# A trunk of four mixers and 32 experts: the scan's input projection on PSUM's two idle banks, and the last norm on VectorE alone

## The chip, the cores and the metric

The kernel runs on one core of a Trainium2 chip. The metric is device time in microseconds (us) of one execution. Engines: PE is TensorE (PEld its weight loads), DVE is VectorE, ACT is ScalarE, POOL is GpSimd, SP is SyncE; a "q" behind a name is that engine's instruction queue (SPq L269 issues most weight loads).

## The reference

One layer, 256 tokens of width 1024, float32. Four branches mix the tokens, a gated sum merges them, and a sparse layer of 32 experts (top 4 of 32, weights of 1024 x 2048 and 1024 x 1024 for each expert) follows. Both sub-layers end in a layer norm.

```
proj   = x @ W_in                       # columns go to the branches and gates
br0    = sparse attention(q, ckv, ...)  # ckv = rms_norm(latents); index scores
                                        # relu(q_idx . k_idx) weighted per head,
                                        # the top 64 keys of each query
br1    = gate_b * conv3(gate_c * u)
br2    = s5 scan(u_scan)                # 32 groups of 16 channels, 64 complex states
br3    = 4-head attention into 256 memory tokens
h      = LN(alpha * x + (sum_r sigmoid(g_r) * (br_r @ W_branch[r])) @ W_o)
out    = LN(alpha * h + MoE(h))         # LN: (y - mu) * rsqrt(var + eps) * g + b
```

## The kernel before

The program is written as generators for the branches (`main`, `select`, `scan_part`, `memory` and others) that are advanced in turn. A scheduler then sets the order of the instructions on each engine from its own costs, so an edit in one place can move instructions in others. The order on an engine is fixed when the program is built; at run time each instruction waits for its inputs and for a free buffer, and everything behind it on its engine waits with it.

There are two long stages. In the dense stage (0 to about 400 us of the span) the projections are computed with the token block as the moving operand. Weights come as float32 by DMA, 1 MB at a time; each piece of 1024 x 128 is split by ScalarE (L320) and VectorE (L325) into a high and a low part, and each product takes three matmuls of 256 columns (`mm3`, L386 to L388), 8 times over, so that 24 matmuls make one half of a tile `[128, 512]`. Between them stand the small matmuls of the branches. In the expert stage (about 400 to 1300 us) 16 pairs of experts are streamed: L1500 and L1518 multiply, L1529 and L1530 scatter the result back to the tokens, L1534 adds it up.

All matmul results lie in PSUM, which has 8 banks of 512 float32 columns in each partition. The kernel hands them out by three pools that go round: `P` has 4 banks, `PT` (transposes) 2, and `PD` 2. The names that matter here:

- `pckv` (L1036, two tiles of `P`): the latents of the sparse attention before their norm. ScalarE computes the root of their mean square (L1039, result `rr`), VectorE inverts it (L1044) and multiplies it in (L1046, `latents()`), TensorE transposes the result (`pct`, L1051).
- `prl` (L820, tiles of `P`): index scores of `select`, taken through a Relu by ScalarE (L825), weighted and summed by VectorE (L832, L834); L840 and L841 find the largest.
- `pu` (L386 to L388, copied out by L1059): the scan's input projection, two tiles of two halves each, 96 matmuls in all. `projs` (L956) takes the bank from `P`. The generator calls `latents()` after the first tile.
- `warm` (L417), the only user of `PD` before the projection; the next is `pkt` (L696, L697) of `scan_part`, which comes behind it on TensorE.
- `scan_part` in four parts: `pkt`, `pe` (transposes, L707, copied out by ScalarE at L708), `pV` (L719, copied at L722), then VectorE's rotation and scan (L724 to L730), `py` (copied out at L747). Two parts run interleaved.
- `memory`: `pml` (scores), VectorE's row maximum (L926, L927), ScalarE's exponent (L929), VectorE's division (L931, L933), transposes `pmt` (copied out at L941), `pmo` (L945, product with the values).
- The tail: after the last pair VectorE aggregates the moments (L1745), ScalarE takes a root (L1746), VectorE inverts it (L1747) and forms `nm` (L1748). The output is four blocks of 128 rows x 512 columns. In each, VectorE takes columns 0 to 399 (`LNV`) in two operations (L1755, L1759); ScalarE normalises the other 112 (L1756) and GpSimd multiplies by the gain (L1757) and adds the bias (L1758). Each block leaves by its own DMA (L1760).

Of the kernel before, what the change touches and what calls it, by code (L numbers as in the profile page):

```python
# [13 lines left out]
FT = mybir.dt.float32  # L14
# [3 lines left out]
AF = mybir.ActivationFunctionType  # L18
OP = mybir.AluOpType
# [11 lines left out]
SC = 8  # L31
# [22 lines left out]
PLACES_AT = 3  # L54
ROWS_AT, SPLIT_AT = 1, 5
RESID = 4
LNV = 400
POOL_MIN = 4096
AHEAD = 2
AHEAD_W = 1  # L60
# [111 lines left out]
def tile_trunk(ctx, tc, a, out):  # L172
    nc = tc.nc
    PE, V, S, G = nc.tensor, nc.vector, nc.scalar, nc.gpsimd
# [5 lines left out]
    keep = ctx.enter_context(tc.tile_pool(name="keep", bufs=1))  # L180
# [10 lines left out]
    def P(nm):  # L191
        return ps.tile([128, 512], FT, name=nm, tag="pp", bufs=4)

    def PT(nm):
        return ps.tile([128, 512], FT, name=nm, tag="pt", bufs=2)

    def PD(nm):
        return ps.tile([128, 512], FT, name=nm, tag="pd", bufs=2)
# [161 lines left out]
    def take(i, half=None):  # L360
        unit = i, None if i in whole else half
        at = split_order.index(unit)
        n = AHEAD_W if i in whole else AHEAD
        for j in split_order[at:at + 1 + n]:
            if j not in ready:
                ready[j] = W(*j)
        return ready[unit] if half == unit[1] else Half(ready[unit], half)
# [22 lines left out]
    def projT(dst, w, c0, xx, m=128):  # L390
        for k in range(w.k):
            mm3(dst, w.h[:, k, c0:c0 + m], w.l[:, k, c0:c0 + m], xx.h[:, k, :], xx.l[:, k, :], k == 0, k == w.k - 1)
# [61 lines left out]
    def small(shape, nm, bufs=2):  # L454
        return keep.tile(shape, FT, name=nm, bufs=bufs)
# [71 lines left out]
    p = PT("pvc")  # L527
# [425 lines left out]
        res["br3"] = oX  # L953


    def projs(ids, xx, nm, put):  # L956
        for c, i in enumerate(ids):
            p = P(nm)
            for j in range(2):
                w = take(i, j)  # L960
                projT(p[:, j * 256:(j + 1) * 256], w, 0, xx)
                w.done()
            put(c, p)
            yield
# [4 lines left out]
    def main():  # L969
        res["kTm"] = B(128, MH, T)  # L970
        for c, _ in enumerate(projs(ID_K, mT, "pk", copy_to(res["kTm"]))):
            if c == 0:
                norm_in()
            yield
        vM = B(128, 2, MH * MD)
        for c, i in enumerate(ID_V):
            w = take(i)
            p = P("pv")
# [25 lines left out]
        p = P("pqi")  # L1004
# [9 lines left out]
        p = P("pki")  # L1014
# [16 lines left out]
        ss, r = small([128, 2], "ss", 1), small([128, 2], "rr", 1)  # L1031
        pl_ = [P("pckv") for _ in range(2)]
        for b in range(2):
            o = pl_[b][:, :136]
# [8 lines left out]
        def latents():  # L1043
            V.reciprocal(r, r)  # L1044
            for b in range(2):
                V.scalar_tensor_tensor(ckv.ap[:, b, :], pl_[b][:, :LAT], r[:, b:b + 1], kvg.ap, op0=OP.mult, op1=OP.mult)  # L1046
            for t in (wcw, kvg, sq, hF):
                t.free()
            p = PT("pct")
            for b in range(2):  # L1050
                PE.transpose(p[:, b * 128:(b + 1) * 128], ckv.ap[:, b, :], ident)  # L1051
            S.copy(ckvT.ap, p[:, :T])
            res.update(ckv=ckv, ckvT=ckvT)
# [4 lines left out]
        res.update(io_blk=io_blk, U=U, io2=carve(io_blk[1], (128, SC, 8, GN), *[(128, 8, GN), (128, 8, NJ + 1)] * 2))  # L1058
        for c, _ in enumerate(projs(ID_S, hX, "pu", lambda c, p: S.copy(  # L1059
                uP.ap[:, :, 2 * c:2 * c + 2, :].rearrange("p s m j -> p m j s"),  # L1060
                p.rearrange("p (m j s) -> p m j s", m=2, s=SC)))):
            if c == 0:
                latents()
            yield
        hN.free()
        res["uP"] = uP
        mqT = B(128, MH, T)
        yield from projs(ID_M, hX, "pmq", copy_to(mqT))
        res["mqT"] = mqT
        qT = B(128, 4, T)  # L1070
# [5 lines left out]
        for c2 in range(2):  # L1076
# [11 lines left out]
            for i in range(2):  # L1088
                c = c2 * 2 + i
                V.tensor_scalar(cv.ap[:, i, :], vv.ap[:, i, 0:T], cw(c, 0), cw(c, 3), op0=OP.mult,  # L1090
                                op1=OP.add)
                for k in (1, 2):
                    V.scalar_tensor_tensor(cv.ap[:, i, :], vv.ap[:, i, k:k + T], cw(c, k), cv.ap[:, i, :],
                                           op0=OP.mult, op1=OP.add)
# [8 lines left out]
        for n, r in enumerate((1, 3, 2, 0)):  # L1103
            if r == 2:
# [3 lines left out]
                for c in range(4):  # L1108
                    w = take(ID_GL, c // 2)
                    p = P("pgl")  # L1110
# [15 lines left out]
            for d2 in range(KC // 2):  # L1126
                p = P("pg")
# [7 lines left out]
                p = P("pbr")  # L1135
# [3 lines left out]
                m = mg.ap[:, 2 * d2:2 * d2 + 2, :].rearrange("p a t -> p (a t)")  # L1139
# [115 lines left out]
    for _ in main():  # L1255
        ahead()
        for nm in list(bgs):
            step(nm)
# [62 lines left out]
    for b in range(2):  # L1321
        mu, r, nm = mv1[:, b, 0:1], r1[:, b:b + 1], nm1[:, b:b + 1]
# [15 lines left out]
        p = PD("prk")  # L1338
# [401 lines left out]
                          {RESID: residual, RESID + 4: norm_rows}[e0]() if e0 in (RESID, RESID + 4) else None, e0 == 0, ln2 if final else None, after, behind, overflow)  # L1740
            ga = after

    mv2, r2, nm2 = keep.tile([128, 2, 2], FT, name="mv2"), small([128, 2], "r2", 1), small([128, 2], "nm2", 1)
    for b in range(2):
        V.bn_aggr(mv2[:, b], ln2[b].st)  # L1745
    S.activation(r2, mv2[:, :, 1], AF.Sqrt, bias=eps_t[:, 0:1], scale=1.0)  # L1746
    V.reciprocal(r2, r2)  # L1747
    V.scalar_tensor_tensor(nm2, mv2[:, :, 0], -1.0, r2, op0=OP.mult, op1=OP.mult)  # L1748
    for b in range(2):
        mu, r, nm = mv2[:, b, 0:1], r2[:, b:b + 1], nm2[:, b:b + 1]  # L1750
        for c in range(2):
            y = o = yacc[0].ap[:, b, c * 512:(c + 1) * 512]
            g_, b_ = (gb2[0].ap[:, i, c * 512:(c + 1) * 512] for i in range(2))
            va, vb = slice(0, LNV), slice(LNV, 512)
            V.scalar_tensor_tensor(o[:, va], y[:, va], mu, g_[:, va], op0=OP.subtract, op1=OP.mult)  # L1755
            S.activation(o[:, vb], y[:, vb], AF.Identity, bias=nm, scale=r)  # L1756
            G.tensor_tensor(o[:, vb], o[:, vb], g_[:, vb], op=OP.mult)  # L1757
            G.tensor_tensor(o[:, vb], o[:, vb], b_[:, vb], op=OP.add)  # L1758
            V.scalar_tensor_tensor(o[:, va], o[:, va], r, b_[:, va], op0=OP.mult, op1=OP.add)  # L1759
            nc.sync.dma_start(out[0, b * 128:(b + 1) * 128, c * 512:(c + 1) * 512], o)  # L1760


# [10 lines left out]
```

## Time and profile before

| what | value |
|---|---|
| time, median of 3 runs (lowest to highest) | 1317.6 us (1317.01 to 1318.38) |
| the profiled execution's own time, and its span | 1318.57 us, 1316.7 us |
| granted TensorE clock, mean over the span | 0.992 of 2.4 GHz |
| busy share of the span: PE, PEld, DVE, ACT, POOL | 92%, 51%, 36%, 24%, 8% |
| DMA over the span | 463.38 MB, mean 352 GB/s |

The rows below come from that one profiled execution. Times in them are microseconds from the start of the span. The busy shares are means over stages that are limited by different things, so a share of the whole span says little of one stage. Of a matmul the pitch (start of one to start of the next) tells what it costs in a row of matmuls, since they overlap: a 256-column matmul is listed with 0.28 us and starts every 0.12 us. The same holds for VectorE, whose operations are listed longer than their pitch.

### The profile page before, as it was taken

To read this page: it belongs to the slowest core of one execution; us is meant where nothing else is said; L and a number is where in the kernel's file an instruction comes from. 1 tells how busy PE (TensorE), PEld (TensorE's weight loads), DVE (VectorE), ACT (ScalarE), POOL (GpSimd) and SP (SyncE) were. 2 spreads that over 40 slices of the span, in tenths; PEclk is the share of its full clock that TensorE was granted. 3 is DMA by queue.
4 is the path that set the end of the run, shared out by engine and by line. 5 is a ranking of instruction groups with operands and counts; after the bars stand their busy time and mean duration, and the time that the engine had idled before them with its cause. 6 is when DMAs were issued, how large, how long until landed. Compare 5 with 4: busy or idle time off the path is not lost. (4 is left out here: it accounts for less than half of the span.)

```text
span 1316.7 us, 17368 instructions
## 1 busy us (share of the span) xinstructions
PE 1214.9 (92%) x6928; PEld 669.2 (51%) x6928; DVE 469.8 (36%) x972; ACT 319.6 (24%) x639; POOL 107.3 (8%) x158
## 2 busy tenths in 40 slices
PE   8799999999999999999999999898989898899984
PEld 8699999889853333333343333333333333333321
DVE  5896976755632133221212213021221212130214
ACT  4735545544422111011211102011010102020101
POOL 1103020246110000000000000000000000000001
PEclk9999999999999999999999999999999999999998
DMA  9816458974889999999999999999999999999993
GB/s 249 273 36 172 130 144 291 292 249 164 319 324 412 419 420 419 419 420 419 420 419 418 420 419 421 420 419 420 419 421 418 420 420 418 421 419 420 412 413 131
DMA packets 115238, 463.38 MB, mean 352 GB/s; under 512 B 19304, under 2 KB 54192, under 8 KB 68016
## 3 DMA queue, kind: packets, MB, share of 16 engines
q1 hardware_dynamic: 112512, 456.37, 87.6%
q0 software_dynamic: 2608, 5.83, 1.7%
q8 instruction: 57, 0.93, 0.3%
q14 instruction: 29, 0.24, 0.0%
q10 hardware_dynamic: 32, 0.01, 0.0%
HBM read 459.09 MB, written 3.08 MB: 351 GB/s over the span
## 5 line engine op out<-in xcount | busy, mean ns | idle before, releaser
L1500 PE MATMUL hp<-slab,slab 128*64 128x512 f32 x2048 | 484.7, 597 | 31.2 <-DMA slab<-in_w_up_dram 30.8
L1500 PEld LDWEIGHTS hp<-slab,slab 128*64 128x64 f32 x2048 | 157.6, 137 | 321.5 <-issue 238.5
L1518 PE MATMUL dp<-slab,slab 128*64 128x512 f32 x1024 | 232.3, 597 | 2.2 <-ACT slab L1515 1.2
L1518 PEld LDWEIGHTS dp<-slab,slab 128*64 128x64 f32 x1024 | 72.4, 137 | 127.3 <-issue 120.9
L325 DVE TENSOR_TENSOR slab<-slab,slab 128x1024 fp32r<-128x1024 f32 (+1 forms) x90 | 110.3, 1235 | 55.8 <-ACT slab L320 50.5
L320 ACT CAST slab<-slab 128x1024 fp32r<-128x1024 f32 x90 | 92.6, 1048 | 78.9 <-DMA slab<-in_w_in_dram 16.5
L1391 ACT ACTIVATE slab<-pxs,pcol 128x128 f32<-128x128 f32 x128 | 48.0, 457 | 235.2 <-PE pxs L1386 225.1
L1491 DVE CAST slab<-id 128x64 fp32r<-128x64 f32 x34 | 5.1, 192 | 221.3 <-PE hp L1494 212.5
L1377 POOL TENSOR_SCALAR slab<-slot_i,slot 128x64 f32<-128x64 f32 x32 | 13.9, 453 | 803.6 <-PE pta L1513 701.6
L388 PE MATMUL pg<-slab,slab 128*128 128x256 f32 x256 | 74.4, 291 | 0.0
L386 PE MATMUL pg<-slab,slab 128*128 128x256 f32 x256 | 74.3, 290 | 0.0
L387 PE MATMUL pg<-slab,slab 128*128 128x256 f32 x256 | 73.6, 288 | 0.0
L1386 PEld LDWEIGHTS pxs<-slab,slab 128*128 128x128 f32 x512 | 59.7, 192 | 25.7 <-issue 23.5
L1457 ACT CAST slab<-psg 128x256 fp32r<-128x256 f32 x16 | 6.0, 372 | 255.5 <-PE psg L1455 255.5
L1386 PE MATMUL pxs<-slab,slab 128*128 128x128 f32 x512 | 65.9, 282 | 1.1 <-DVE slab L1377 0.7
L1443 DVE TENSOR_SCALAR slab<-hp 128x256 f32<-128x256 f32 x64 | 27.0, 422 | 76.5 <-PE pta L1513 76.5
L1534 DVE TENSOR_TENSOR slab<-slab,psc 128x512 f32<-128x512 f32 x60 | 38.6, 684 | 43.7 <-PE psc L1530 43.7
L386 PEld LDWEIGHTS pg<-slab,slab 128*128 128x128 f32 x256 | 49.8, 194 | 2.0 <-issue 1.5
L388 PEld LDWEIGHTS pg<-slab,slab 128*128 128x128 f32 x256 | 49.9, 195 | 1.1 <-issue 1.1
L387 PEld LDWEIGHTS pg<-slab,slab 128*128 128x128 f32 x256 | 49.8, 194 | 0.3 <-issue 0.2
L1513 PE MATMUL pta<-ident,slab 128*128 128x128 f32 x128 | 26.5, 290 | 24.2 <-ACT slab L1515 24.0
L1515 ACT COPY slab<-pta 128x256 f32<-128x256 f32 x64 | 23.9, 375 | 94.3 <-PE pta L1513 94.3
(446 smaller groups left out, 1533.8 us busy)
## 6 DMA issues: line engine op xcount, KB each, us to landing
slab<-in_w_up_dram SPq DMA_DIRECT2D x256, 1024.0 KB, 19.9
slab<-in_w_down_dram SPq DMA_DIRECT2D x126, 1024.0 KB, 19.9
slab<-in_w_in_dram SPq DMA_DIRECT2D x29, 1024.0 KB, 6.6
slab<-in_w_branch_dram SPq DMA_DIRECT2D x8, 1024.0 KB, 7.3
slab<-in_w_mem_kv_dram SPq DMA_DIRECT2D x4, 1024.0 KB, 10.9
slab<-in_w_o_dram SPq DMA_DIRECT2D x4, 1024.0 KB, 8.1
slab<-kp_d POOLq DMA_DIRECT2D x32, 64.0 KB, 3.9
slab<-in_w_down_dram SPq DMA_DIRECT2D x4, 512.0 KB, 16.6
```

Source lines behind the costliest of these rows:

```text
L320: ins = S.copy(r_(hi[:, sl]), src[:, sl])
L325: ins = eng.tensor_tensor(r_(lo[:, p0:p1]), src[:, p0:p1], hi[:, p0:p1], op=OP.subtract)
L386: PE.matmul(dst, lh, rh, start=first, stop=False)
L387: PE.matmul(dst, lh, rl, start=False, stop=False)
L388: PE.matmul(dst, ll, rh, start=False, stop=last)
L1386: PE.matmul(p[:, i * 128:(i + 1) * 128], hN.ap[:, b, k * 128:(k + 1) * 128], self.S2.ap[:, b].rearrange("p e s -> p (e s)"), start=b == 0 ...
L1391: S.activation(self.xs.ap[:, k, :], p[:, i * 128:(i + 1) * 128], AF.Identity, bias=col(3, k), scale=col(2, k))
L1443: V.tensor_scalar(l.ap, hv[:, :, :, 1], LIMIT, -LIMIT, op0=OP.min, op1=OP.max)
L1500: PE.matmul(hp[nb][e * 64:(e + 1) * 64, :], xs[:, k, e * CAP:(e + 1) * CAP], w, start=start, stop=k == KC - 1, skip_group_check=True)
L1513: PE.transpose(p[:, j * 128:(j + 1) * 128], l.ap[:, j, :], ident)
L1518: PE.matmul(dp[nb][e * 64:(e + 1) * 64, :], aT.ap[:, k, e * 64:(e + 1) * 64], w, start=k == 0, stop=k == KC - 1, skip_group_check=True)
L1534: V.tensor_tensor(y, y, p, op=OP.add)
```

## The change

Two edits. `projs` gets an argument for the pool of its banks, and the scan's input projection passes `PD` instead of the default `P`. In the tail VectorE handles all 512 columns of each block; ScalarE's and GpSimd's shares and the small operation that forms `nm` are gone, as is the constant `LNV`.

```diff
-    def projs(ids, xx, nm, put):
+    def projs(ids, xx, nm, put, bank=P):
         for c, i in enumerate(ids):
-            p = P(nm)
+            p = bank(nm)
...
         for c, _ in enumerate(projs(ID_S, hX, "pu", lambda c, p: S.copy(
                 uP.ap[:, :, 2 * c:2 * c + 2, :].rearrange("p s m j -> p m j s"),
-                p.rearrange("p (m j s) -> p m j s", m=2, s=SC)))):
+                p.rearrange("p (m j s) -> p m j s", m=2, s=SC)), PD)):
...
-    V.scalar_tensor_tensor(nm2, mv2[:, :, 0], -1.0, r2, op0=OP.mult, op1=OP.mult)
...
-            va, vb = slice(0, LNV), slice(LNV, 512)
-            V.scalar_tensor_tensor(o[:, va], y[:, va], mu, g_[:, va], op0=OP.subtract, op1=OP.mult)
-            S.activation(o[:, vb], y[:, vb], AF.Identity, bias=nm, scale=r)
-            G.tensor_tensor(o[:, vb], o[:, vb], g_[:, vb], op=OP.mult)
-            G.tensor_tensor(o[:, vb], o[:, vb], b_[:, vb], op=OP.add)
-            V.scalar_tensor_tensor(o[:, va], o[:, va], r, b_[:, va], op0=OP.mult, op1=OP.add)
+            V.scalar_tensor_tensor(o, y, mu, g_, op0=OP.subtract, op1=OP.mult)
+            V.scalar_tensor_tensor(o, o, r, b_, op0=OP.mult, op1=OP.add)
             nc.sync.dma_start(out[0, b * 128:(b + 1) * 128, c * 512:(c + 1) * 512], o)
```

The line numbers of the changed kernel are one lower from the deleted constant on (L325 of before is L324 there), and lower by more in the tail. TensorE's order around `pu` is the same in both programs: `pckv`, `pc`, `prl`, `pu`. The scheduler's new times move instructions further on, at three places.

The first is VectorE before the third and fourth memory heads, at about 131 to 135 us of the span. `slab_1002` is the rotation and scan of one scan part, `slab_1490` a weight slab being split, `slab_1288` the block that holds the index scores, `slab_1750` the next scan part's first product; L926 takes the row maximum of the memory scores. Before:

```order
L834 SCALAR_TENSOR_TENSOR slab_1288<-slab_1288,wix 128x256
L684 TENSOR_TENSOR slab_1750<-slab_122 128x1024
L325 TENSOR_TENSOR slab_1490<-slab_1435,slab_1489 128x1024
L834 SCALAR_TENSOR_TENSOR slab_1288<-slab_1288,wix 128x256
L926 TENSOR_REDUCE mx<-pml 128x2
```

Now:

```order
L683 TENSOR_TENSOR slab_1750<-slab_122 128x1024
L324 TENSOR_TENSOR slab_1490<-slab_1435,slab_1489 128x1024
L725 SCALAR_TENSOR_TENSOR slab_1002<-slab_1002 128x256
L324 TENSOR_TENSOR slab_1490<-slab_1435,slab_1489 128x1024
L659 SCALAR_TENSOR_TENSOR slab_1002<-slab_1002,slab_121 64x256
L660 SCALAR_TENSOR_TENSOR slab_1002<-slab_1002,slab_121 64x256
L833 SCALAR_TENSOR_TENSOR slab_1288<-slab_1288,wix 128x256
L728 TENSOR_TENSOR slab_1002<-slab_1002,slab_121 128x256
L833 SCALAR_TENSOR_TENSOR slab_1288<-slab_1288,wix 128x256
L729 TENSOR_TENSOR slab_704<-slab_1002 128x8x32
L833 SCALAR_TENSOR_TENSOR slab_1288<-slab_1368,wix,slab_1288 128x256
L925 TENSOR_REDUCE mx<-pml 128x2
```

The row maximum (L926, now L925) stands behind one more weight split and two more of the weighted sums than before; the scan's operations on `slab_1002` have moved behind the split too, but stood ahead of the maximum in both.

The second place is TensorE in the third and fourth scan part, at about 164 to 168 us. `slab_1750` and `slab_1760` are the two parts' first products; `pbr` and `pg` are projections. Before:

```order
L387 MATMUL pbr<-slab_1287,slab_1934 128x256
L707 MATMUL pe<-ident,slab_1760 128x128 x8
L719 MATMUL pV<-slab_703,slab_1750 128x32 x4
L719 MATMUL pV<-slab_703,slab_1760 128x32 x3
L388 MATMUL pg<-slab_196,slab_1777 128x256
```

Now:

```order
L386 MATMUL pbr<-slab_1287,slab_1934 128x256
L718 MATMUL pV<-slab_703,slab_1750 128x32 x8
L706 MATMUL pe<-ident,slab_1760 128x128 x8
L718 MATMUL pV<-slab_703,slab_1760 128x32 x4
L856 MATMUL pkh<-slab_612 128x256
L387 MATMUL pg<-slab_196,slab_1777 128x256
```

All `pV` matmuls of the one part now stand ahead of the other part's transposes `pe`; on ScalarE the copy of that `pV` (L722) has moved with them, ahead of the copies of `pe` (L708).

The third is VectorE in the tail, where `mv` and `r` are the mean and the inverse root. Before:

```order
L1755 SCALAR_TENSOR_TENSOR slab_4317<-slab_4317,mv_8421,slab_5172 128x400
L1747 RECIPROCAL r_8422<-r_8422 128x2
L1755 SCALAR_TENSOR_TENSOR slab_4317<-slab_4317,mv_8421,slab_5172 128x400
L1748 SCALAR_TENSOR_TENSOR nm_8423<-mv_8421,r_8422 128x2
L1759 SCALAR_TENSOR_TENSOR slab_4317<-slab_4317,r_8422,slab_5172 128x400 x2
L1755 SCALAR_TENSOR_TENSOR slab_4317<-slab_4317,mv_8421,slab_5172 128x400 x2
L1759 SCALAR_TENSOR_TENSOR slab_4317<-slab_4317,r_8422,slab_5172 128x400 x2
```

Now:

```order
L1752 SCALAR_TENSOR_TENSOR slab_4317<-slab_4317,mv_8421,slab_5172 128x512
L1746 RECIPROCAL r_8422<-r_8422 128x2
L1752 SCALAR_TENSOR_TENSOR slab_4317<-slab_4317,mv_8421,slab_5172 128x512
L1753 SCALAR_TENSOR_TENSOR slab_4317<-slab_4317,r_8422,slab_5172 128x512 x2
L1752 SCALAR_TENSOR_TENSOR slab_4317<-slab_4317,mv_8421,slab_5172 128x512 x2
L1753 SCALAR_TENSOR_TENSOR slab_4317<-slab_4317,r_8422,slab_5172 128x512 x2
```

Eight operations of 400 columns became eight of 512; ScalarE's four and GpSimd's eight operations on the other 112 columns have left their engines.

## Rows read from the trace of the kernel before

**Rows 1.** What each engine did in four stretches: start and end, length, then busy time and count of PE, PEld, DVE, ACT and POOL, the granted clock as a share of 2.4 GHz, the share of the DMA engines and GB/s. The first is just before `pu`, the second between `pu` and the memory heads, the third the dense stage further on, the last the expert stage.
```profile
58.00:63.00 5.00, 0.59 (x8) 0.40 (x8) 5.00 (x15) 2.55 (x6) 0.15 (x2) 0.94 0.05 23
74.00:100.00 26.00, 25.95 (x245) 25.37 (x241) 25.35 (x48) 11.63 (x20) 0.67 (x3) 1.00 0.21 62
320.00:340.00 20.00, 20.00 (x169) 20.00 (x168) 12.86 (x16) 8.95 (x12) 11.06 (x11) 1.00 0.36 127
500.00:1000.00 500.00, 469.70 (x2218) 185.10 (x2215) 103.86 (x256) 70.97 (x176) 7.84 (x18) 1.00 1.01 419
```

**Rows 2.** TensorE's waits: who waited, for whom, us in total, times, the longest.
```profile
PE hp L1500 <- DMA slab<-in_w_up_dram: 30.8, 30, 1.5
PE pu L386 <- ACT slab L825: 7.1, 1, 7.1
```

**Rows 3.** TensorE in order of time around `pu`: start, us, what, and in brackets the idle time before it and what ended it.
```profile
57.88 0.71 PE L820 MATMUL prl<-slab 32*128 32x128 f32 x8
65.72 0.58 PE L386 MATMUL pu<-slab,slab 128*128 128x256 f32 x1 [7.13 <-ACT slab L825]
...
69.09 0.36 PE L386 MATMUL pu<-slab,slab 128*128 128x256 f32 x1
...
70.00 0.28 PE L387 MATMUL pu<-slab,slab 128*128 128x256 f32 x1
70.12 0.28 PE L388 MATMUL pu<-slab,slab 128*128 128x256 f32 x1
...
73.11 0.38 PE L1051 MATMUL pct<-ident,slab 128*128 128x128 f32 x2
```

**Rows 4.** ScalarE in order of time, before the Relu that `pu` waits for.
```profile
62.78 1.28 ACT L1039 ACT_TABLE_LOAD   x1
...
64.27 1.05 ACT L634 COPY slab<-pc 128x512 f32<-128x512 f32 x2
65.21 0.79 ACT L825 ACTIVATE slab<-prl 128x128 f32<-128x128 f32 x4
```

**Rows 5.** VectorE in order of time, up to the normalised latents.
```profile
65.10 0.16 DVE L1044 RECIPROCAL rr<-rr 128x2 f32<-128x2 f32 x1
...
66.90 0.35 DVE L1046 SCALAR_TENSOR_TENSOR slab<-pckv,rr,slab 128x128 f32<-128x128 f32 x1
...
67.76 0.35 DVE L1046 SCALAR_TENSOR_TENSOR slab<-pckv,rr,slab 128x128 f32<-128x128 f32 x1
```

**Rows 6.** Engines' work (columns as in rows 1) in two stretches in which the granted clock is lower.
```profile
65.50:69.20 3.70, 3.48 (x16) 3.48 (x17) 3.62 (x8) 0.50 (x4) 0.00 (x0) 0.50 0.00 0
168.00:172.00 4.00, 4.00 (x23) 4.00 (x23) 4.00 (x13) 1.99 (x2) 2.27 (x5) 0.57 0.36 81
```

**Rows 7.** VectorE in order of time ahead of and at the third memory head.
```profile
119.65 1.22 DVE L325 TENSOR_TENSOR slab<-slab,slab 128x1024 fp32r<-128x1024 f32 x1 [3.91 <-ACT slab L320]
...
133.21 1.22 DVE L325 TENSOR_TENSOR slab<-slab,slab 128x1024 fp32r<-128x1024 f32 x1
134.34 0.48 DVE L834 SCALAR_TENSOR_TENSOR slab<-slab,wix 128x256 f32<-128x256 f32 x1
134.74 0.69 DVE L926 TENSOR_REDUCE mx<-pml 128x2 f32<-128x512 f32 x1
```

**Rows 8.** ScalarE in order of time, from that head's exponent to the copy that `pmo` waits for.
```profile
136.01 0.47 ACT L929 ACTIVATE slab<-pml,mx 128x256 f32<-128x256 f32 x1 [3.07 <-DVE mx L927]
...
138.09 1.99 ACT L320 CAST slab<-slab 128x1024 fp32r<-128x1024 f32 x2
140.00 2.99 ACT L747 COPY slab<-py 32x256 f32<-32x256 f32 x8
143.01 1.07 ACT L941 COPY slab<-pmt 128x512 f32<-128x512 f32 x2
```

**Rows 9.** TensorE in order of time, at `pmo` and in the third and fourth scan part.
```profile
143.65 2.00 PE L945 MATMUL pmo<-slab,slab 128*128 128x256 f32 x8 [0.77 <-ACT slab L941]
...
164.25 0.28 PE L387 MATMUL pbr<-slab,slab 128*128 128x256 f32 x1
165.93 1.06 PE L707 MATMUL pe<-ident,slab 128*128 128x128 f32 x8 [1.40 <-DVE slab L686]
166.83 1.74 PE L719 MATMUL pV<-slab,slab 128*128 128x32 f32 x14
```

**Rows 10.** The tail in order of time, VectorE, ScalarE and GpSimd.
```profile
1304.50 0.62 DVE L1755 SCALAR_TENSOR_TENSOR slab<-slab,mv,slab 128x400 f32<-128x400 f32 x1
1304.62 0.29 ACT L1746 ACTIVATE r<-mv,eps_t 128x2 f32<-128x2 f32 x1 [2.95 <-DVE mv L1745]
1305.04 0.16 DVE L1747 RECIPROCAL r<-r 128x2 f32<-128x2 f32 x1
...
1306.81 1.50 DVE L1755 SCALAR_TENSOR_TENSOR slab<-slab,mv,slab 128x400 f32<-128x400 f32 x2
1308.23 1.49 DVE L1759 SCALAR_TENSOR_TENSOR slab<-slab,r,slab 128x400 f32<-128x400 f32 x2
...
1310.96 0.42 POOL L1758 TENSOR_TENSOR slab<-slab,slab 128x112 f32<-128x112 f32 x1
```

**Rows 11.** The tail's operations by line: count, then shortest, median and longest in ns, first and last start.
```profile
L1755 DVE SCALAR_TENSOR_TENSOR slab<-slab,mv,slab x4: 615/702/793, 1304.5 to 1307.5; 128x400 f32<-128x400 f32 x4
L1757 POOL TENSOR_TENSOR slab<-slab,slab x4: 419/746/772, 1306.4 to 1310.5; 128x112 f32<-128x112 f32 x4
```

More of the change, by code (lines that the diff above doesn't have):

```diff
@@ L56 @@
 RESID = 4
-LNV = 400
 POOL_MIN = 4096
@@ L1741, in tile_trunk @@
             ga = after
-    mv2, r2, nm2 = keep.tile([128, 2, 2], FT, name="mv2"), small([128, 2], "r2", 1), small([128, 2], "nm2", 1)
+    mv2, r2 = keep.tile([128, 2, 2], FT, name="mv2"), small([128, 2], "r2", 1)
     for b in range(2):
@@ L1747, in tile_trunk @@
     V.reciprocal(r2, r2)
-    V.scalar_tensor_tensor(nm2, mv2[:, :, 0], -1.0, r2, op0=OP.mult, op1=OP.mult)
     for b in range(2):
-        mu, r, nm = mv2[:, b, 0:1], r2[:, b:b + 1], nm2[:, b:b + 1]
+        mu, r = mv2[:, b, 0:1], r2[:, b:b + 1]
         for c in range(2):
```

## The prediction

> **What bounds the kernel now.** I read the stretches first [rows 1]. Between 500 and 1000 us the DMA engines are fully busy (share 1.01, 419 GB/s): there the transfer of the expert weights sets the pace. In the dense stage it does not: at 320 to 340 us the DMA share is 0.36 and TensorE is busy 20.00 of 20 us. From 74 to 100 us TensorE (25.95 of 26 us) and VectorE (25.35 of 26) are both full. So what shortens TensorE's chain in the dense stage starts the expert stream earlier by as much, unless VectorE, or a slab that is not yet free, takes the gain back on the way.
>
> Next the waits [rows 2]. The largest single wait of TensorE is the one that the change goes for: 7.1 us, once, `pu` behind the Relu L825. The others are made of many small ones (hp, 30.8 us in 30). In order of time [rows 3] `prl` ends at 57.88 + 0.71 = 58.59 and `pu` starts at 65.72, after 7.13 us idle. ScalarE shows why [rows 4]: the Relu that empties the banks of `prl` starts at 65.21, behind a table load (62.78) and the copies L634. `pu` needs none of that data, only a bank, and `PD` has had two idle ones since the start. The tail is read last [rows 10]: the last operation ahead of the last output DMA is GpSimd's at 1310.96 + 0.42 = 1311.38.
>
> The sum is made against the profiled execution's own 1318.57 us (1316.7 of span and 1.87 around it); the median is 1317.6, so savings are taken off that at the end.
>
> **A, the wait before `pu`: 5.0 us gained.** With a bank at hand `pu` can start at 58.59. Its first tile is 2 x 24 = 48 matmuls at a pitch of 0.12 (70.00 to 70.12) [rows 3], 5.8 us, so it is done at 64.3. Next on TensorE stand the transposes `pct`, and they need the normalised latents. VectorE finishes these with the second L1046 at 67.76 + 0.35 = 68.11 [rows 5]. Nothing of the change makes that earlier: VectorE is busy 5.00 of 5 us from 58 to 63 [rows 1], its order up to there is unchanged, and it doesn't wait for `pu`. So `pct` starts at 68.1 instead of 73.11: 5.0 us, not 7.1. A new hole of 68.1 − 64.3 = 3.8 us takes the place of the old one; it is what is late next. Bounds: 5.0 above (VectorE), and below 0, if VectorE's full stretch from 74 to 100 us absorbs the lead. I take 5.0, because later VectorE does wait: it is idle for 3.91 us at 119.65, for a ScalarE cast that follows TensorE [rows 7].
>
> **B, the clock behind the hole: 1.5 lost.** In the 3.7 us from 65.50 the granted clock is 0.50, that is 1.2 GHz, behind the 7.13 us hole; in the 4 us from 168 it is 0.57, mostly 1.2 GHz, shortly behind a hole of 1.40 us [rows 6, 9]. The first cost is read off the pitches: 15 steps from 65.72 to 69.09 take 3.37 us instead of 15 x 0.12 = 1.8, so 1.5 [rows 3]. In A this cost already went with the old hole (the 48 matmuls were counted at full speed). The new 3.8 us hole lies between the two old ones in length and both of those were followed by the lower clock, so I charge 1.5 once more. Bounds 0 and 3.0 (twice that). The Trainium skill ("TensorE: Matmul & The Clock Gate", section "What's actually happening") speaks against this edit's full gain: it says that throttling is the default and activity lifts it. Both old holes agree; by that rule a shortened hole isn't a removed one and the sum below stands; without it the charge goes, and the time is R1's.
>
> **C, VectorE's order before the memory head: 1.9 lost.** The row maximum L926 stands behind one more split L325 (pitch 134.34 − 133.21 = 1.13) and two more L834 (pitch 134.74 − 134.34 = 0.40 each), 1.9 us in all [rows 7]. Behind it hang, one after the other and in an order that hasn't changed, ScalarE's exponents (136.01), its casts L320 (138.09), the `py` copies (140.00) and the copy L941 (143.01) [rows 8] and on TensorE `pmo`, which even now waits 0.77 us for that copy [rows 9]. A chain with a wait at its end has no slack, so the 1.9 comes off TensorE's lead. Bounds 0 (if some of the 1.99 us of casts can run ahead of waiting exponents, which the order doesn't let them, or if the lead is so large that nobody waits) and 2.3 (a second of the `slab_1002` group late too, 0.4). I take 1.9.
>
> **D, the hole at 165 us: 1.0 gained.** TensorE is idle 1.40 us before the transposes `pe` at 165.93, which wait for VectorE (L686) [rows 9]. All eight `pV` of the other part, ready by then, now stand ahead; 14 `pV` in 1.74 us make 8 about 1.0. ScalarE's copy of that `pV` now stands before the copies of `pe`, for which the second part's `pV` wait. The copy's 256 columns cost less than the 0.5 of a 512-column copy (two L941 in 1.07) [rows 8]; I take it as hidden in the 0.4 us of the hole that are left. Bounds 0 (no room, since VectorE is the late one and the order makes no difference) and 1.4 (all of the hole). The lower clock at 168 us I leave as it is: some hole of 0.4 us remains.
>
> **E, the tail: 1.5 gained.** VectorE does eight operations of 512 columns instead of 400. A 400-column operation with no GpSimd work beside it has a pitch of 0.54 (1304.50 to 1305.04) [rows 10], a 256-column one 0.40 [rows 7]: 0.14 us for 144 columns, 0.001 a column, so 0.54 + 112 x 0.001 = 0.65 for 512. The inverse root at 1305.04 + 0.16 has its input since 1304.62 + 0.29 and costs 0.07. From 1304.50 that is 8 x 0.65 + 0.07 = 5.3, and 0.1 more until the last one's end: 1309.9, against 1311.38, 1.5 gained. Beside GpSimd the same 400-column operation had a pitch of 1308.23 − 1306.81 = 1.42 for two, 0.71 each. If that pitch held without GpSimd, 512 columns would take 0.82 and the end be at 1304.50 + 6.6 + 0.1 = 1311.2, a gain of 0.2; if width cost nothing (0.54), 2.4. I take 1.5, from the rows without GpSimd. The span of slow and fast is seen in [rows 11]: 615 to 793 ns for the same VectorE operation, and 419 to 772 for GpSimd's. The Trainium skill ("SBUF — State Buffer", section "Who interferes with whom") has the reason: a VectorE operation with two inputs in SBUF and a GpSimd one that reads SBUF share a port pair, of which one holds the other off. The rows agree; by that rule the pitch is 0.65 and the tail gains 1.5, without it 0.82 and 0.2.
>
> **The sum:** 5.0 − 1.5 − 1.9 + 1.0 + 1.5 = 4.1. Against the profiled execution 1318.57 − 4.1 = 1314.5; against the median 1317.6 − 4.1 = **1313.5 us**.
>
> **Rivals.**
> - R1, the clock is not lost a second time: with the 165 us hole filled and the new one at 64.3 being shorter than the old, one of the two low-clock stretches goes, +1.5. 5.6 gained, 1312.0. For it: the hole that is filled is the shorter. Against: 3.8 us is long beside 1.40.
> - R2, the dense lead is given back: somewhere before the expert stream a DMA or a slab holds it (from 320 to 340 us DMA is not full, which speaks against; the stream is bound by transfer from its start, which speaks for it where loads cannot be issued earlier). Only the tail remains, 1.5: 1316.1. The change as a whole failing to free `pu` (the `PD` banks held by something that I don't see) gives the same time.
> - R3, the tail is not faster (pitch 0.82): 4.1 − 1.3 = 2.8, 1314.8.
> - R4, slower than before: VectorE is the bound from 58 to 145 us. Its queue does not move earlier, so A and B fall to nothing, while L926 is 1.9 later. The wait at `pmo` grows from 0.77 to 2.7 us, and like the 1.40 us hole brings the lower clock, 1.5. Sum −1.9 − 1.5 + 1.0 + 1.5 = −0.9: 1318.5. It decides if VectorE's 3.91 us of idle time before 119.65 goes; with a lead of 3.5 us on TensorE and nothing added in front of that row the idle time stays about as long, which speaks against it.
>
> **How the numbers follow.** Forecast 0.46, R1 0.20, R2 0.18, R3 0.08, R4 0.08. The forecast's own range is 1311.9 to 1315.1 (B, C and E can each be off by 1 to 1.5, mostly not together). The range 1311.2 to 1316.5 takes in R1 to R3, and leaves out R4 and the ends of the others, 2 in 10 together. A measurement of this kernel can't tell less than 0.2%, 2.6 us, from no change: faster means below 1315.0, slower above 1320.2. Faster is most of the forecast (0.40), R1 (0.20) and half of R3 (0.04), with 0.01 of R2: 0.65. Slower is what of R4 goes beyond its time, and what none of the cases names: 0.05. The same is the rest, 0.30.
>
> **What would show it.** A: `pu` at 58.6 of the span and no wait for L825, and `pct` at about 68.1 behind a hole of 3.8 us, ended by VectorE's L1046. B: 1.2 GHz in the granted clock behind `pct`, as behind the hole of before; full clock there means R1. C: a wait of `pmo` for L941 no shorter than 0.77, and a lead of TensorE that falls by 1.9 between 120 and 145 us. D: a hole before `pe` of about 0.4. E: first and last of VectorE's eight operations 4.6 us apart at a pitch of 0.65, the last DMA 1.5 us nearer to the moments (L1745) than before. The prediction is wrong if the start of the expert stream lies within 1 us of before (R2), if VectorE has no idle time around 119 us (R4), or if an operation of the tail takes 0.8 us (R3).

## The result: 22.6 us faster, where 4.1 were forecast

The changed kernel takes 1295.15 us (median of 4 runs, 1294.02 to 1296.65), the kernel before 1317.74 (4 runs, 1317.01 to 1318.38). The ratio is 0.983 with a 95% interval of 0.982 to 0.984. The time lies outside the range on record. The profiled execution took 1294.02 us, with a span of 1292.2.

The first view to read again is that of the stretches, with the same bounds as [rows 1] and [rows 6]:

```profile
58.00:63.00 5.00, 5.00 (x45) 4.88 (x46) 5.00 (x13) 4.36 (x9) 0.03 (x1) 1.00 0.01 3
65.50:69.20 3.70, 3.16 (x26) 2.76 (x27) 3.62 (x8) 3.02 (x7) 0.00 (x0) 1.00 0.00 0
74.00:100.00 26.00, 25.94 (x263) 24.89 (x263) 25.78 (x56) 11.16 (x19) 2.26 (x6) 1.00 0.30 94
500.00:1000.00 500.00, 474.19 (x2249) 186.06 (x2247) 105.63 (x258) 70.63 (x175) 7.84 (x18) 1.00 1.01 427
```

TensorE is busy all through 58 to 63 us, where it was idle for most of the time: that is the edit at work. In this execution it also runs at full clock from 65.5 us on. The last row is the surprise: in the expert stage, where the change touches nothing, the DMA share is 1.01 as before but the rate is 427 GB/s instead of 419. The loads of `w_up` land after 19.5 us (median) instead of 19.9:

```profile
slab<-in_w_up_dram SPq DMA_DIRECT2D x256, 1024.0 KB, 19.5
```

TensorE in order of time, around `pu` and at the first expert pair's first matmul of L1493, which is L1494 in the kernel before:

```profile
58.49 0.39 PE L385 MATMUL pu<-slab,slab 128*128 128x256 f32 x1
...
65.57 0.30 PE L1050 MATMUL pct<-ident,slab 128*128 128x128 f32 x1 [1.06 <-ACT slab L319]
66.34 0.33 PE L1050 MATMUL pct<-ident,slab 128*128 128x128 f32 x1 [0.47 <-DVE slab L1045]
...
396.10 0.73 PE L1493 MATMUL hp<-slab 64*128 64x512 f32 x4
```

The same matmul before:

```profile
403.45 0.73 PE L1494 MATMUL hp<-slab 64*128 64x512 f32 x4
```

And the tail in order of time, to be held against [rows 10]:

```profile
1282.77 0.19 DVE L1744 BATCH_NORM_AGGREGATE mv<-ln20s 128x2 f32<-128x12 f32 x1
...
1283.01 0.73 DVE L1752 SCALAR_TENSOR_TENSOR slab<-slab,mv,slab 128x512 f32<-128x512 f32 x1
1283.13 0.30 ACT L1745 ACTIVATE r<-mv,eps_t 128x2 f32<-128x2 f32 x1 [2.96 <-DVE mv L1744]
1283.66 0.16 DVE L1746 RECIPROCAL r<-r 128x2 f32<-128x2 f32 x1
...
1285.71 1.41 DVE L1752 SCALAR_TENSOR_TENSOR slab<-slab,mv,slab 128x512 f32<-128x512 f32 x2
1287.03 1.41 DVE L1753 SCALAR_TENSOR_TENSOR slab<-slab,r,slab 128x512 f32<-128x512 f32 x2
```

The kernel before has its first aggregation of the moments, L1745, at this row:

```profile
1304.26 0.19 DVE L1745 BATCH_NORM_AGGREGATE mv<-ln20s 128x2 f32<-128x12 f32 x1
```

With these rows the two spans, 1316.7 and 1292.2, part as follows:

| stretch | before | now | less by |
|---|---|---|---|
| start to the first L1494 (L1493) of the experts | 403.45 | 396.10 | 7.4 |
| from there to the first aggregation of the moments | 900.8 | 886.7 | 14.1 |
| from there to the end of the last computing operation | 7.1 (1311.38) | 5.7 (1288.44) | 1.5 |
| from there to the end of the span | 5.3 | 3.8 | 1.6 |

I had forecast 2.6, 0, 1.5 and 0. The spans of these two executions lie 24.5 us apart, the medians 22.6: the profiled execution of before took 1318.57, longer than the four runs of it above, and that of now was the shortest of its four. The first row depends on this most: another execution of the changed kernel (e0 below) has the first L1493 at 399.39, so 4.1 less and not 7.4, and the same 886.7 us behind it.

### The profile page after: what moved, and what is told of

It reads as the page before. It is cut to its first block, busy times and chain, and to the rows that moved or that the text cites. A ratio compares the mean times of both kernels' runs of the same rounds, so it can differ in the third digit from the quotient of the medians.

```text
span 1292.2 us, 17353 instructions
## 1 busy us (share of the span) xinstructions
PE 1209.1 (94%) x6928; PEld 667.6 (52%) x6928; DVE 468.7 (36%) x971; ACT 318.1 (25%) x635; POOL 102.9 (8%) x150
## 5 line engine op out<-in xcount | busy, mean ns | idle before, releaser
L324 DVE TENSOR_TENSOR slab<-slab,slab 128x1024 fp32r<-128x1024 f32 (+1 forms) x90 | 109.9, 1233 | 48.5 <-ACT slab L319 43.1
L1376 POOL TENSOR_SCALAR slab<-slot_i,slot 128x64 f32<-128x64 f32 x32 | 13.9, 452 | 791.1 <-PE pta L1512 689.6
## 6 DMA issues: line engine op xcount, KB each, us to landing
slab<-in_w_up_dram SPq DMA_DIRECT2D x256, 1024.0 KB, 19.5
slab<-in_w_down_dram SPq DMA_DIRECT2D x126, 1024.0 KB, 19.5
```

The lines of the kernel that those rows point to most:

```text
L324: ins = eng.tensor_tensor(r_(lo[:, p0:p1]), src[:, p0:p1], hi[:, p0:p1], op=OP.subtract)
```

## The experiments

They ran in three groups of four, each beside runs of the kernel before on the same chip, whose medians were 1317.61 (e0 to e3), 1317.46 (e4 to e7) and 1317.34 us (e8 to e12). "Ratio" is to these, with its 95% interval; the GB/s are those of the stretch from 500 to 1000 us; "first slab" is the byte in each partition at which the built program puts the first of the 25 weight slabs of 8192 bytes.

| run | us (lowest to highest) | ratio | GB/s | first slab |
|---|---|---|---|---|
| e1_bank_only | 1315.03 (1313.61 to 1315.41) | 0.9968 to 0.9988 | 419 | 24096 |
| e2_tail_only | 1297.34 (1296.73 to 1298.78) | 0.9831 to 0.9864 | 427 | 24064 |
| e3_lnv384 | 1317.62 (1316.37 to 1319.21) | 0.9990 to 1.0009 | 419 | 24096 |
| e0_after_again | 1296.61 (1292.23 to 1301.22) | 0.9805 to 0.9870 | 427 | 24064 |
| e4_after_base_back | 1311.42 (1309.63 to 1312.34) | 0.9933 to 0.9963 | 419 | 24096 |
| e5_before_base_only | 1301.85 (1300.52 to 1302.16) | 0.9862 to 0.9892 | 427 | 24064 |
| e6_before_base128 | 1313.67 (1312.72 to 1315.34) | 0.9959 to 0.9983 | 421 | 24192 |
| e7_tail_base_back | 1314.50 (1314.12 to 1316.12) | 0.9969 to 0.9987 | 419 | 24096 |
| e8_before_base256 | 1301.33 (1300.49 to 1302.65) | 0.9864 to 0.9894 | 427 | 24320 |
| e9_before_base224 | 1317.44 (1316.89 to 1318.97) | 0.9991 to 1.0010 | 419 | 24288 |
| e11_latents_later | 1292.40 (1291.59 to 1293.31) | 0.9798 to 0.9825 | 426 | 24064 |
| e12_gpsimd_last | 1298.10 (1296.04 to 1299.04) | 0.9836 to 0.9866 | 427 | 24064 |

### Which edit makes the stream faster?

My first theory was D: the earlier dense stage starts the stream in another rhythm. Its rivals: P, the rate is a property of the program as loaded, and C, it is one of the chip or the hour. The first run is the change without its tail:

```diff
-    def projs(ids, xx, nm, put):
+    def projs(ids, xx, nm, put, bank=P):
...
-                p.rearrange("p (m j s) -> p m j s", m=2, s=SC)))):
+                p.rearrange("p (m j s) -> p m j s", m=2, s=SC)), PD)):
```

> Only the bank edit; the tail of before. The profile of the changed kernel shows three gains: TensorE is 7.4 us ahead at the start of the expert stream, the stream moves 427 instead of 419 GB/s (about 15 us over 800 us), and the tail is shorter by 1 to 2 us. Theory D (the earlier dense stage gives the stream another start, and with it the higher rate): this kernel has both the lead and the rate, 1296 to 1297 us. Theory P (the rate belongs to the program as it is loaded, its size or where its data lie, not to what the edit does): the lead of 5 to 7.4 us for certain, the rate at either level, so 1310 to 1313 or 1296 to 1297.

1315.03 us, with the stream at 419 GB/s. D is dead: this kernel had the lead and not the rate.

```profile
398.92 0.73 PE L1494 MATMUL hp<-slab 64*128 64x512 f32 x4
```

The second run has the tail of the change and nothing else:

```diff
-            va, vb = slice(0, LNV), slice(LNV, 512)
...
+            V.scalar_tensor_tensor(o, y, mu, g_, op0=OP.subtract, op1=OP.mult)
+            V.scalar_tensor_tensor(o, o, r, b_, op0=OP.mult, op1=OP.add)
```

> Only the tail edit. Nothing before the tail changes its order. Theory D: stream at 419 GB/s, only the tail is shorter, 1316 us. Theory P: the rate may go to 427 GB/s although the edit runs only behind the stream, then 1298 to 1300 us.

1297.34 us at 427 GB/s: the edit that runs behind the stream makes the stream faster. The third changes one number of the tail, with all operations kept:

```diff
-LNV = 400
+LNV = 384
```

> An edit that does next to nothing: 384 instead of 400 columns of each block for VectorE in the tail of the kernel before. Theory D: 419 GB/s, 1317 to 1319 us. Theory P: either 1317 to 1319, or 427 GB/s and about 1300.

1317.62 us at 419 GB/s. The fourth is the changed kernel again.

> The changed kernel once more, on the chip of the three others. If the rate belongs to the program, its stream runs at 427 GB/s and the time is 1294 to 1297 us, beside 1317 to 1318 for the kernel before. If it belongs to the chip or the hour (theory C), kernel before and changed kernel have the same rate here and stand about 8 us apart.

1296.61 us at 427 GB/s, on the chip on which the kernel before took 1317.61. C falls. This kernel's four runs lie 9 us apart. The mean granted clock goes part of the way with them (0.995 in the shortest, 0.992 in the two longest); the cause of the rest is open.

Not every edit to the tail does it, so I looked at what the tail edit changes outside the tail. It deletes `nm2`, a tile of 8 bytes a partition that takes 32, and the slabs lie behind the small tiles, last in each partition, so that nothing else moves with them. The built programs show it:

```
before   mv2 at 24000, r2 at 24032, nm2 at 24064, first slab at 24096 = 94 x 256 + 32
changed  mv2 at 24000, r2 at 24032,               first slab at 24064 = 94 x 256
```

All slabs follow at steps of 8192, so the start of every weight row that lands has moved. How long the 8 KB packets took, counted from the trace's packet records between 600 and 700 us:

```
kernel                 ns (packets)
before                 313 (2893)  320 (924)  314 (353)  309 (347)  315 (263)  321 (141)
changed                309 (5196)  774 (2)    312 (1)    311 (1)
```

The mean falls from 314.9 to 309.3 ns, by 1.8%; the rate rises from 419 to 427 GB/s, by 1.9%.

### Is it where the slabs start?

Theory S: yes. Theory G: no, it is the work taken off GpSimd and ScalarE. e4 is the changed kernel plus one tile that nothing uses:

```diff
     mv2, r2 = keep.tile([128, 2, 2], FT, name="mv2"), small([128, 2], "r2", 1)
+    small([128, 2], "pad", 1)
```

> The changed kernel with one unused tile of 32 bytes a partition, which puts the weight slabs back to where the kernel before has them: first slab at byte 24096 of each partition (32 past a multiple of 256) instead of 24064 (a multiple of 512). No instruction changes. Theory S (the rate of the stream is set by the byte at which the slabs start, since the deleted tile nm2 moved them by 32 bytes): 419 GB/s and 8 KB packets of 313 to 320 ns again, 1313 to 1314 us (1317.6 less 2.6 for the bank edit and 1.5 for the tail). Theory G (what counts is the work that GpSimd and ScalarE no longer have in the tail, or another start of the stream): 427 GB/s and 1294 to 1297 us.

```profile
500.00:1000.00 500.00, 469.16 (x2209) 183.11 (x2206) 103.83 (x254) 70.60 (x175) 7.84 (x18) 1.00 1.01 419
```

1311.42 us at 419 GB/s: the same instructions with the slabs 32 bytes further on, 15 to 16 us slower (1295.15 in the result above, 1296.61 in e0). e5 goes the other way, with the tail of before:

```diff
-    mv2, r2, nm2 = keep.tile([128, 2, 2], FT, name="mv2"), small([128, 2], "r2", 1), small([128, 2], "nm2", 1)
+    mvn, r2 = keep.tile([128, 2, 3], FT, name="mv2"), small([128, 2], "r2", 1)
+    mv2, nm2 = mvn[:, :, 0:2], mvn[:, :, 2]
```

> The kernel before with nm2 laid into the spare bytes of mv2's 32: same work, same operations, first slab at byte 24064. Theory S: 427 GB/s, 18 us off the stream and about 1 off the dense stage, 1298 to 1300 us. Theory G: 419 GB/s and 1317 to 1318 us.

The stretch, and the two ends of the stream as in the table above:

```profile
500.00:1000.00 500.00, 474.29 (x2250) 184.92 (x2248) 105.29 (x256) 70.72 (x175) 7.87 (x18) 1.00 1.01 427
```

```profile
400.40 0.73 PE L1494 MATMUL hp<-slab 64*128 64x512 f32 x4
...
1287.28 0.19 DVE L1746 BATCH_NORM_AGGREGATE mv<-ln20s 128x2 f32<-128x12 f32 x1
```

1301.85 us, 15.6 less than before, with GpSimd and ScalarE at work in the tail as ever. The stream takes 1287.28 − 400.40 = 886.9 us, the 886.7 of the changed kernel; the dense stage, which has its own loads, is 3.0 shorter (403.45 − 400.40). All profiles agree on the stream, counted from the first L1494 (L1493) to the moments: 900.4 to 900.8 us in the six with slabs at 32 or 224 past a multiple of 256, 886.1 to 886.9 in the seven with slabs at one, 897.5 in e6. S stands in both directions and G falls.

Which starts are good? Three more unused tiles in the kernel before, of 96, 224 and 192 bytes:

```diff
+    small([128, 24], "pad", 1)
...
+    small([128, 56], "pad", 1)
...
+    small([128, 48], "pad", 1)
```

> The kernel before with an unused tile of 96 bytes: first slab at byte 24192, which is 128 past a multiple of 256 and a multiple of 64. Theory S with a grain of 64 bytes: as in the base-only run, about 1299 us. Theory S with a grain of 256 bytes: packets longer than 309 ns, 1315 to 1320 us, or above if the cost grows with the offset. Theory G: 1317 to 1318 us.

> The kernel before with an unused tile of 224 bytes: first slab at byte 24320, a multiple of 256 and not of 512. If the grain of the slab's start is 256 bytes: 427 GB/s and 1300 to 1303 us, as with the start at 24064 (1301.85). If it is 512: 419 to 421 GB/s and 1313 to 1318 us.

> The kernel before with an unused tile of 192 bytes: first slab at byte 24288, 224 past a multiple of 256. If what a start off the grain costs grows with the bytes past it (as the Trainium skill's page on DMA, DMA: Bandwidth & Descriptors, section How a descriptor splits into AXI transactions, has it for reads): the slowest of all, 414 to 416 GB/s, 1322 to 1328 us. If any start off the grain costs about the same: 419 to 421 GB/s, 1313 to 1318 us.

128 past a multiple of 256: 1313.67 us, 421 GB/s; at a multiple of 256: 1301.33, 427; 224 past: 1317.44, 419, as with 32 past. The packets of 600 to 700 us again:

```
first slab             ns (packets)
24192 = 128 past       309 (1328)  314 (760)  312 (643)  311 (450)  313 (426)  318 (353)
24288 = 224 past       313 (2808)  320 (788)  309 (352)  321 (262)  316 (256)  314 (194)
24320 = a multiple     309 (5192)  774 (2)    315 (1)    314 (1)
```

So of the starts tried, only the multiples of 256 have the full rate, and 512 isn't needed. The Trainium skill ("DMA: Bandwidth & Descriptors", section "How a descriptor splits into AXI transactions") says that a transfer is cut into transactions of 256 bytes and that one which doesn't begin on such a boundary is charged for extra bytes. The grain agrees with these runs. The size does not: by that account, which is told of reads, the cost rises with the bytes past the boundary, whereas 224 past costs what 32 past does, 16 us over e8, and 128 past less, 12. Other starts, such as 64 past, were not tried. Why a write into SBUF is slower off the boundary no run here shows.

### What is the tail worth by itself?

e7 is e2 with the unused tile of e4, so the tail edit with the slabs where they were.

> The tail edit alone, with the unused tile of 32 bytes: first slab at 24096 as before. This measures the tail by itself. Theory S: 419 GB/s and 1316 us, a gain of 1.5 (between 0.2 and 2.4). Theory G: as in the run of the tail edit alone, 1297 us.

```profile
1302.90 0.19 DVE L1746 BATCH_NORM_AGGREGATE mv<-ln20s 128x2 f32<-128x12 f32 x1
...
1305.85 1.41 DVE L1754 SCALAR_TENSOR_TENSOR slab<-slab,mv,slab 128x512 f32<-128x512 f32 x2
1307.17 1.41 DVE L1755 SCALAR_TENSOR_TENSOR slab<-slab,r,slab 128x512 f32<-128x512 f32 x2
```

1314.50 us, 3.0 less than before (1.7 to 4.1 by the interval), more than the 2.4 that I had as the upper bound. From the aggregation to the last operation's end it takes 5.7 us (1302.90 to 1308.58) instead of 7.1. The other 1.5 lie behind: the span of 1312.4 goes on for 3.8 us, that of before for 5.3, although the output's last packet has landed 1.7 us behind the last operation in both. Of the profiles so far, all that end on a GpSimd operation go on for 5.3 us (before, e1, e3, e5, e6, e8 and e9), all that end on VectorE for 3.8 (the changed kernel, e0, e2, e4 and e7, and e11 below). In e5 the last row is

```profile
1293.98 0.42 POOL L1759 TENSOR_TENSOR slab<-slab,slab 128x112 f32<-128x112 f32 x1
```

in a span of 1299.7. To test that, e12 puts one tiny GpSimd operation behind the tail of the changed kernel:

```diff
             nc.sync.dma_start(out[0, b * 128:(b + 1) * 128, c * 512:(c + 1) * 512], o)
+    G.tensor_copy(r2, o[:, 0:2])
```

> The changed kernel with one tiny GpSimd copy of two columns behind VectorE's last operation in the tail; no output depends on it. Theory C (closing the program takes about 1.5 us longer behind a last operation on GpSimd than behind one on VectorE, which is why the tail edit gained 3.0 and not 1.5): the span goes on for about 5.3 us behind that copy instead of 3.8 behind VectorE's last, so 1.5 us and the copy's own 0.2 to 0.5 more, 1297 us. If the longer ending of the kernel before was the last output transfer's wait for GpSimd: no change, 1295 us.

```profile
1289.78 1.41 DVE L1753 SCALAR_TENSOR_TENSOR slab<-slab,r,slab 128x512 f32<-128x512 f32 x2
1290.55 0.99 SPq L1754 DMA_DIRECT2D out_dram<-slab  x2
1291.25 0.19 POOL L1755 COPY r<-slab 128x2 f32<-128x2 f32 x1 [136.97 <-DVE slab L1753]
```

The span is 1296.7: 5.3 us behind the copy (1291.44) and 5.5 behind VectorE (1291.19), where the changed kernel has 3.8. Nothing waits for the copy, so the ending itself is 1.5 us longer when GpSimd finishes last. The median, 1298.10, is higher too, but its interval meets that of e0; the verdict rests on the ends of the spans. What the program does in its ending the trace has no rows for.

### Can the rest of the hole go?

e11 is the changed kernel with the latents' norm and transposes called one step later, so that the second tile of `pu` fills the wait for VectorE:

```diff
-            if c == 0:
+            if c == 1:
                 latents()
```

> The changed kernel with the norm of the latents and their transposes called behind the second tile of the scan's projection instead of the first; same slabs. TensorE then does not wait for VectorE's L1045 between the two tiles (1.5 us of holes in the profile of the changed kernel, 2.5 to 3.2 in the two other kernels with the bank edit, two of which also ran at 1.2 GHz behind it). If TensorE's lead there reaches the expert stream: 1.5 to 4 us less, 1291 to 1294 us. If VectorE, which is full from 74 to 100 us, takes it back: 1294 to 1297 us as before.

```profile
58.00:71.00 13.00, 13.00 (x114) 12.63 (x111) 12.86 (x32) 9.29 (x21) 0.00 (x0) 1.00 0.00 1
```

TensorE is busy 13.00 of 13 us at full clock, and the first L1493 stands at 394.30 instead of 396.10 (399.39 in e0). The mean granted clock is 0.995 in all five runs, where the eight of the changed kernel have 0.992 to 0.995. At 1292.40 us this is the fastest kernel of the study, 2.8 below the changed kernel's 1295.15 (4.2 below its 1296.61 in e0); the intervals of the ratios, 0.9798 to 0.9825 and 0.9816 to 0.9839, still meet, so the size is uncertain.

## Why the prediction was wrong, step by step

**The step that failed** is in the first paragraph: that in the expert stage "the transfer of the expert weights sets the pace". It does, but I took its rate, 419 GB/s, as given for both kernels, and the sum has no term for it. The cause stood in the diff: I took the deletion of `nm2` for a small operation that goes, not for 32 bytes ahead of the slabs that go too. The slab start is worth 15.6 us (e5) or 16.0 (e8), about seven tenths of the whole. Of the 17.0 us between the spans of before and e5, 13.9 lie in the stream (900.8 − 886.9) and 3.0 in the dense stage. No rival had it either.

**A and the sum of the bank edit** hold. e1 measured 2.6 us by the medians (1.6 to 4.2 by the interval); A to D added up to 5.0 − 1.5 − 1.9 + 1.0 = 2.6. That the two are equal is luck in part, as B and D below show. Its trace shows the steps:

```profile
66.98 0.30 PE L1051 MATMUL pct<-ident,slab 128*128 128x128 f32 x1 [2.48 <-DVE slab L1046]
67.75 0.33 PE L1051 MATMUL pct<-ident,slab 128*128 128x128 f32 x1 [0.47 <-DVE slab L1046]
68.00 0.77 PE L820 MATMUL prl<-slab 32*128 32x128 f32 x8
68.70 0.58 PE L386 MATMUL pu<-slab,slab 128*128 128x256 f32 x1
69.09 0.41 PE L387 MATMUL pu<-slab,slab 128*128 128x256 f32 x1
...
116.93 1.99 PE L945 MATMUL pmo<-slab,slab 128*128 128x256 f32 x8
...
141.50 1.99 PE L945 MATMUL pmo<-slab,slab 128*128 128x256 f32 x8 [1.80 <-ACT slab L941]
...
163.92 1.07 PE L707 MATMUL pe<-ident,slab 128*128 128x128 f32 x8
165.29 1.08 PE L719 MATMUL pV<-slab,slab 128*128 128x32 f32 x8 [0.29 <-ACT slab L708]
```

- A: behind `pu` a new hole, ended by VectorE's L1046 as forecast, 2.48 and 0.47 us instead of 3.8. I had let both transposes wait for the second L1046, and the first of them needs the first only; the second starts at 67.75, for which I had 68.1.
- B: the `pu` matmuls behind it have 0.41 us, the length that they have in the first stretch of [rows 6] in the kernel before, and the granted clock of 67 to 70 us is 0.76; e4 has 0.52 there. In the profile of the changed kernel the holes are 1.06 and 0.47 us and the clock stays at 1.00, but that is one execution. In e0, the same program, and in e12 the first hole is 2.42 and 2.84 us and the clock of 67 to 70 us is 0.50. So the lower clock came in all four profiles with a hole of 2.4 to 2.9 us (e0, e1, e4, e12), as forecast, and not in the two with a shorter one or none (the changed kernel, e11).

The kernel before:

```profile
68.88 0.41 PE L388 MATMUL pu<-slab,slab 128*128 128x256 f32 x1
```

The changed kernel again (e0):

```profile
66.03 0.30 PE L1050 MATMUL pct<-ident,slab 128*128 128x128 f32 x1 [2.42 <-DVE slab L1045]
67.00:70.00 3.00, 3.00 (x17) 2.72 (x17) 2.96 (x6) 2.06 (x6) 0.00 (x0) 0.50 0.00 0
```

- Beside A and B, the slabs' start moves this place too: e5, in which nothing else moved, has the old wait 2.0 us earlier than [rows 3], and the second `pct` starts at 66.3 to 66.8 us in the three profiles of the bank edit with slabs at 24064 that keep the old call of `latents()`, at 67.8 and 68.1 in the two with slabs at 24096. So A's "Nothing of the change makes that earlier" was wrong by 1 to 2 us, for the same reason as the stream.

```profile
63.75 0.58 PE L386 MATMUL pu<-slab,slab 128*128 128x256 f32 x1 [7.13 <-ACT slab L825]
```

- C: `pmo` waits for L941 for 1.80 us instead of 0.77, and the lead over the kernel before falls from 4.0 us (120.88 against 116.93) to 2.2 (143.65 against 141.50), a loss of 1.8 where I had 1.9. The changed kernel has the same wait, 1.80. R4 falls: VectorE's idle time, now before 115.70, is the 3.91 us of [rows 7] again. First the `pmo` of before, then VectorE in e1:

```profile
120.88 2.00 PE L945 MATMUL pmo<-slab,slab 128*128 128x256 f32 x8
```

```profile
115.70 1.22 DVE L325 TENSOR_TENSOR slab<-slab,slab 128x1024 fp32r<-128x1024 f32 x1 [3.91 <-ACT slab L320]
```

- D: the hole before `pe` is gone and one of 0.29 us before `pV` is left, about the 0.4 forecast. The clock is not lowered behind it, which R1 had:

```profile
168.00:172.00 4.00, 4.00 (x36) 4.00 (x35) 4.00 (x9) 0.00 (x0) 3.28 (x7) 1.00 0.50 139
```

But the filled hole isn't shown to be the reason. Eight profiles of kernels without the bank edit have the old hole of about 1.4 us at this place, and only two of them (before and e3) the lower clock behind it. e7 has the hole and full clock:

```profile
166.44 1.07 PE L707 MATMUL pe<-ident,slab 128*128 128x128 f32 x8 [1.39 <-DVE slab L686]
168.00:172.00 4.00, 4.00 (x35) 4.00 (x35) 4.00 (x12) 2.23 (x3) 1.71 (x5) 1.00 0.28 63
402.33 0.73 PE L1494 MATMUL hp<-slab 64*128 64x512 f32 x4
```

So the lead of e1 at the first L1494 is 403.45 − 398.92 = 4.5 us against the execution of before, and 3.4 against e7 (402.33), which has the same dense stage. The medians of e1 say 2.6, and their interval takes in the 3.4 and R1's 4.1 too, so how much of the lead comes from the clock stays open.

**E** was right in what it counted: a pitch of 0.65 (1283.01 to 1283.66), the operations 1.5 us shorter. It was too small by the 1.5 us of the ending, which it left out because I followed the path only to the last output transfer. The whole tail measured 3.0.

**The sum of the parts as measured:** 15.6 (e5) + 2.6 (e1) + 3.0 (e7) = 21.2, against 22.6 for the change in the result above and 21.0 in e0. Without the slabs' move the change gives 1317.46 − 1311.42 = 6.0 (e4; 4.9 to 8.8 by its interval), where I had forecast 4.1. The ending's 1.5 is most of that difference, and the rest is inside the interval. With the slabs where they were the time would have been 1317.6 − 6.0 = 1311.6, just inside the range on record.

## What to carry to other kernels

When an edit adds or deletes a buffer, compare the addresses of all others before and after: in a stage bound by transfers, 32 bytes that moved the landing place decided more than all the instructions that were saved. Put the destinations of large loads on multiples of 256 bytes (shown here for rows of 8 KB), and where GB/s changes at an unchanged DMA share of 1.0, look at the time of a packet before the schedule. Where a stretch depends on the clock, look at a second profile of the same program before you give the cause. On the path to the end, follow the span to its last microsecond, the ending behind the last engine included.

## What the runs showed of the hardware that I had not expected

- An 8 KB packet into SBUF takes 309 ns with its rows at multiples of 256 bytes, and mostly 313 to 320 at 32 or 224 past, with the DMA engines fully busy (share 1.01): 427 against 419 GB/s from 500 to 1000 us.
- The program's ending is 5.3 us long behind a last operation on GpSimd and 3.8 behind one on VectorE, whether or not anything waits for the GpSimd operation.
- Behind a hole of 2.4 to 2.9 us TensorE ran at 1.2 GHz for some us in all four profiles that have one; behind one of 1.4 us in two of eight, although the dense stage's program and the hole were the same.
